# Local attention: both heads' probabilities transposed and copied first, their value products then issued in turn

## The chip, the cores and the metric

The kernel runs on one core of a Trainium2 chip. What counts is the device time of one execution in microseconds; the median of three runs of the kernel before is 2738.02 us (2737.78 to 2738.24). A core has five engines that run side by side and wait for each other through semaphores: TensorE (PE; its weight loads are listed as PEld), VectorE (DVE), ScalarE (ACT), GpSimd (POOL) and SyncE (SP, which here issues the DMAs). Each engine takes its own instructions in the order in which they stand in its queue.

## What is computed

A two-layer encoder block on 1024 tokens of width 1024. Each layer projects the tokens, runs three mixers side by side (differential attention over all keys with six heads, spatial gating, and a windowed attention with six query heads on two key heads), projects back, and adds a gated feed-forward part and a gated embedding part. The change is in the windowed ("local") attention:

```
def window_gqa(q, k, v, sinks, slopes):
    ...
    sc = jnp.where(valid[None, :, None, None], sc, NEG_INF)
    sink = sinks.astype(jnp.float32).reshape(SWA_KV_HEADS, SWA_GROUP)[:, :, None, None]
    m = jnp.maximum(jnp.max(sc, axis=-1, keepdims=True), sink)
    e = jnp.exp(sc - m)
    pr = e / (jnp.sum(e, axis=-1, keepdims=True) + jnp.exp(sink - m))
    o = jnp.einsum('bnkgqc,bnckd->bnqkgd', pr.astype(v.dtype), vb)
```

In the last line the probabilities of a block of 128 queries over its up to 384 keys are multiplied with the values of those keys.

## The kernel before

Tokens are cut into 8 blocks of 128. `swa(t, b)` does the local attention for query block t and two heads at once (g = 0 and 1, that is heads b and b + 3, one for each key head). It is called 24 times in each layer, 48 times in all. A block sees nk = 3 key blocks, the first and the last block nk = 2: 36 units with 384 columns and 12 with 256.

A unit goes through these steps. Scores for both heads on TensorE (L419), a bias, minimum and copy on VectorE (L425), the exponential on ScalarE (L428). Then, head after head: nk transposes of the probabilities on TensorE into a PSUM bank (L434), one copy of that bank to SBUF by ScalarE into a tile named PT (L436), and nk value products on TensorE (L438). A value product has 64 output rows: head 0 uses columns 0 to 63 of TensorE's array, head 1 columns 64 to 127 (in the profile the form 128\*64; a visit of this form is called a 64-column visit below). Each value product is fp32 and shows as two records. At the end the output goes to SBUF (L444), is transposed back (L446) and scaled by VectorE (L447).

`diff` is the differential attention, 48 calls a layer: scores (L481), VectorE (L484), ScalarE (L487), then per half of the keys four transposes (L503), a copy by ScalarE into a PT tile (L505), and value products (L509) that take the two column halves in turn by the key block's parity; L512 to L516 finish it. Its PT tiles, three buffers in all, and the two PSUM banks for transposes (4 and 5) are shared with `swa`.

A loop issues `diff` calls, `swa` calls and projection pieces (L238) by counts; but the order on each engine is made afterwards, by a scheduler that goes over the whole program with its own estimates of time. So an edit to one function moves instructions of its neighbours as well. Matrix products of the output projection (L220) follow at the end of the stage. The two layers have the same order in the parts shown here.

Of the kernel before, what the change touches and what calls it, by code (L numbers as in the profile page):

```python
# [16 lines left out]
AF = mybir.ActivationFunctionType  # L17
# [3 lines left out]
P = 128  # L21
# [36 lines left out]
def encoder_kernel(  # L58
# [7 lines left out]
    nc = tc.nc  # L66
# [6 lines left out]
    def nm(s):  # L73
        uid[0] += 1
        return f"{s}_{uid[0]}"

    def new(tag, shape, dt=F32):
        return sb.tile(shape, dt, tag=tag, name=nm(tag), bufs=BUFS[tag])

    def stat(k):  # L80
        if spos[0] + k > 224:
            spos[0] = 0
        spos[0] += k
        return stats[:, spos[0] - k : spos[0]]
# [4 lines left out]
    def pick(starts, width, hold):  # L89
        ok = [i for i in starts if not held & set(range(i, i + width))]  # L90
        i = min(ok, key=lambda j: max(stamp[j : j + width]))
        for j in range(i, i + width):
            stamp[j] = max(stamp) + 1
            if hold:
                held.add(j)
        return i

    def pbank2(hold=False):
        i = pick(SCORE_BANKS, 2, hold)
        return banks[:, i : i + 2]  # L100

    def pbank(among=range(4, 8), hold=False):
        i = pick(among, 1, hold)
        b = banks[:, i]
        bank_of[id(b)] = (i, b)
        return b
# [3 lines left out]
    def pfree(b):  # L110
        i = bank_of[id(b)][0]
        held.discard(i)
        stamp[i] = max(stamp) + 1
# [188 lines left out]
    for l in range(DEPTH):  # L302
# [40 lines left out]
        def vt(t, c0, n):  # L343
            c0 += (t % 2) * 512
            return V[:, t // 2, c0 : c0 + n]
# [31 lines left out]
        def c_view(t, b):  # L377
            return T(t)[:, 640 + P * b : 768 + P * b]
# [26 lines left out]
        def swa(t, b):  # L405
            k0, k1 = max(0, t - 1), min(NT, t + 2)
            nk = k1 - k0
            off = (k0 - t + 1) * P
            n = nk * P
            nmx, ssum = stat(2), stat(2)  # L410
            pr = new("G", [P, 2, 512])

            nc.gpsimd.tensor_copy(pr[:, :, n : n + 1], nsink[:, b : b + 4 : 3].unsqueeze(2))
            sc2 = pbank2()
            for g in range(2):
                h = b + 3 * g
                sc = sc2[:, g]
                rows = slice(64 * g, 64 * g + 64)
                nc.tensor.matmul(sc[:, :n], c_view(t, b)[rows], ck[0][rows, k0 * P : k1 * P],  # L419
                                 start=True, stop=True)  # L420
            for g in range(2):
                h = b + 3 * g
                sc = sc2[:, g]
                pg = pr[:, g, :n]
                nc.vector.tensor_tensor_reduce(pg, sc[:, :n], wtab[:, off : off + n], SWA_SLOPES[h],  # L425
                                               nsink[:, h : h + 1], ALU.add, ALU.min, nmx[:, g : g + 1])
                pg = pr[:, g, : n + 1]
                nc.scalar.activation(pg, pg, AF.Exp, bias=nmx[:, g : g + 1], scale=-1.0, accum_out=ssum[:, g : g + 1])  # L428
            yield
            po = pbank(AV_BANKS, hold=True)  # L430
            for g in range(2):
                pt = pbank(PT_BANKS)
                for j in range(nk):
                    nc.tensor.transpose(pt[:, j * P : (j + 1) * P], pr[:, g, j * P : (j + 1) * P], ident)  # L434
                pT_ = new("PT", [P, 512])
                nc.scalar.activation(pT_[:, :n], pt[:, :n], AF.Copy)  # L436
                for j in range(nk):
                    nc.tensor.matmul(po[64 * g : 64 * g + 64, 0:P],  # L438
                                     vt(k0 + j, 384 + 64 * g, 64), pT_[:, j * P : (j + 1) * P],
                                     start=(j == 0), stop=(j == nk - 1))  # L440
            rd = stat(2)
            nc.vector.reciprocal(rd, ssum)
            oT = new("O", [P, P])
            nc.scalar.activation(oT, po[:, 0:P], AF.Copy)  # L444
            pb = po[:, 256:384]
            nc.tensor.transpose(pb, oT, ident)  # L446
            nc.vector.tensor_tensor(c_view(t, b).rearrange("p (g d) -> p g d", g=2), pb.rearrange("p (g d) -> p g d", g=2),  # L447
                                    rd.unsqueeze(2).to_broadcast([P, 2, 64]), op=ALU.mult)
            pfree(po)
            yield  # L450
# [191 lines left out]
        for i in range(len(seq) + 2):  # L642
            if i < len(seq):
                h, t = seq[i]
                for hh in STACK_AT.get(i, ()):
                    slots[hh] = [stack(hh, 0), stack(hh, 1)]
                if i == GAINS_AT:
                    gpm = gain("G", g_post_mix, l)
                    gpf = gain("G", g_pre_ffn, l)
                g = diff(h, t, slots[h], i)  # L650
                next(g)
                pend.append((g, h, t))
                if i >= WO_AT:
                    load_wo(1)
                while nf < min(16, FILL_FIRST + 0.558 * (i + 1)):
                    next(fill)
                    nf += 1
                while ns < min(24, 0.629 * (i - 5)):
                    sg = swa(ns % 8, [int(f) for f in FILL if f in "012"][ns // 8])
                    next(sg)  # L660
                    spend.append(sg)
                    ns += 1
            while len(spend) > (1 if ns < 24 else 0):
                next(spend.pop(0))
            while pend and (len(pend) > 1 or i >= len(seq) + (len(pend) < 2)):
                g, h, t = pend.pop(0)
                next(g)
                if h == 5 and t >= MIX_LAG:
                    next(mix_step, None)
                if i >= len(seq):  # L670
                    break
# [254 lines left out]
```

## Time and profile before

| | |
|---|---|
| median of 3 runs | 2738.02 us |
| the profiled execution | 2735.23 us |
| its span | 2733.5 us |
| TensorE busy (PE) | 2675.9 us (98%) |
| weight loads (PEld) | 2154.2 us (79%) |
| VectorE busy | 1745.6 us (64%) |
| ScalarE busy | 1161.8 us (43%) |
| GpSimd busy | 323.1 us (12%) |

The span is the time from the first to the last instruction of the profiled execution. A TensorE matmul's busy time includes the time in which it runs beside the next one, so the busy times of single matmuls add up to more than the time that passes; the start of one block to the start of the next is what it takes. The local attention runs from 220 to 470 us (first layer) and from 1565 to 1805 us (second layer).

### The profile page before, as it was taken

The numbers are of one execution on the slowest core, as the hardware profiler recorded it, in microseconds if no ns is written. First come the engines' busy times: TensorE is split into PE (matmuls) and PEld (weight loads), VectorE is DVE, ScalarE is ACT, GpSimd is POOL, SyncE is SP. The second block draws the span as 40 slices with busy tenths as digits, with TensorE's granted clock in tenths as the row PEclk, the third lists the DMA queues.
The fourth block names the chain that finished last, engine by engine and source line by source line (L and its number), as shares of the span: only waits on it lengthen the run. The fifth ranks groups of instructions, "written<-read, shape, count | busy, mean of one in ns | idle before, by whom it ended". The sixth has DMA issues, their size and how long they took to land.

```text
span 2733.5 us, 35609 instructions
## 1 busy us (share of the span) xinstructions
PE 2675.9 (98%) x13760; PEld 2154.2 (79%) x13760; DVE 1745.6 (64%) x2944; ACT 1161.8 (43%) x1959; POOL 323.1 (12%) x299
## 2 busy tenths in 40 slices
PE   8999999999999999999999999999999999999998
PEld 6887776778888888887878777668788888888877
DVE  5237687568665646768632677866866666466684
ACT  6126788453222323124521577855433222321253
POOL 1002335210000000001100223532000000000010
PEclk9999999999999999999999999999999999999999
DMA  7153402133323214334224323012332232433332
GB/s 238 30 150 93 109 2 70 63 97 90 93 70 93 83 65 154 101 100 143 93 81 110 99 70 94 24 62 78 92 109 82 80 93 67 134 122 110 131 129 80
DMA packets 193465, 258.38 MB, mean 95 GB/s; under 512 B 26512, under 2 KB 142736, under 8 KB 193296
## 3 DMA queue, kind: packets, MB, share of 16 engines
q1 hardware_dynamic: 193296, 256.11, 30.5%
q8 instruction: 108, 1.77, 0.3%
q14 instruction: 61, 0.50, 0.1%
HBM read 195.25 MB, written 60.82 MB: 94 GB/s over the span
## 4 chain that ended last, share of the span: by engine, by line
PE 90%; DVE 6%; DMA 2%; issue 1%; ACT 1%; SPq 0%; POOL 0%; DVEq 0%; POOLq 0%; ACTq 0%
PE banks L714 30%; PE banks L220 17%; PE banks L793 16%; PE banks L238 8%; PE banks L509 3%; PE banks L503 3%; PE banks L481 3%; PE banks L438 2%; PE banks L202 2%; PE banks L266 1%; PE banks L419 1%; PE banks L434 1%; DVE A L196 1%; PE banks L515 1%; DMA raw<-in_w_in_dram 1%
## 5 line engine op out<-in xcount | busy, mean ns | idle before, releaser
L714 PE MATMUL banks<-A,W 128*128 128x512 f32 x3072 | 710.5, 391 | 7.2 <-ACT W L161 4.9
L714 PEld LDWEIGHTS banks<-A,W 128*128 128x128 f32 x3072 | 579.2, 189 | 131.3 <-ACT W L161 6.4
L220 PE MATMUL banks<-W,A 128*128 128x512 f32 x1728 | 420.6, 396 | 12.0 <-ACT A L209 6.4
L220 PEld LDWEIGHTS banks<-W,A 128*128 128x128 f32 x1728 | 322.8, 190 | 81.3 <-ACT A L209 7.6
L799 DVE TENSOR_TENSOR A<-banks,A 128x512 f32<-128x512 f32 x320 | 213.9, 687 | 111.7 <-PE banks L793 111.4
L793 PE MATMUL banks<-W,F 128*128 128x512 f32 x1152 | 263.7, 389 | 0.0
L793 PEld LDWEIGHTS banks<-W,F 128*128 128x128 f32 x1152 | 216.2, 188 | 44.9
L793 PE MATMUL banks<-W,W 128*128 128x512 f32 x960 | 220.0, 389 | 1.8 <-ACT W L161 1.8
L161 ACT ACTIVATE W<-G 128x1024 fp32r<-128x1024 f32 x88 | 92.5, 1060 | 296.8 <-PE banks L714 279.0
L189 POOL TENSOR_TENSOR stats<-stats,neghalf 128x1 f32<-128x1 f32 (+1 forms) x112 | 84.8, 759 | 1095.7 <-DVE stats L187 1094.6
L793 PEld LDWEIGHTS banks<-W,W 128*128 128x128 f32 x960 | 180.1, 188 | 39.4 <-ACT W L161 2.0
L161 ACT ACTIVATE W<-raw 128x1024 fp32r<-128x1024 f32 x92 | 96.7, 1059 | 209.6 <-PE banks L793 100.7
L238 PE MATMUL banks<-A,F 128*128 128x512 f32 x768 | 183.8, 393 | 0.0
L738 DVE TENSOR_TENSOR P<-banks,P 128x512 f32<-128x512 f32 x44 | 30.4, 690 | 219.7 <-PE banks L714 219.7
L238 PEld LDWEIGHTS banks<-A,F 128*128 128x128 f32 x768 | 142.1, 188 | 29.5 <-issue 0.7
L484 DVE CUSTOM_DVE_ANT_0 P<-banks,dist 128x1024 f32<-128x1024 f32 x116 | 139.9, 1218 | 36.2 <-PE banks L481 22.8
L220 PE MATMUL banks<-F,A 128*128 128x512 f32 x576 | 148.0, 400 | 0.7 <-DVE stats L484 0.7
L487 ACT ACTIVATE P<-P,stats 128x1024 f32<-128x1024 f32 x116 | 133.0, 1148 | 28.7 <-DVE stats L484 26.9
L162 DVE TENSOR_TENSOR W<-raw,W 128x1024 fp32r<-128x1024 f32 x80 | 97.6, 1223 | 52.6 <-ACT W L161 52.5
L714 PE MATMUL banks<-A,raw 128*128 128x512 f32 x528 | 126.8, 389 | 0.0
L220 PEld LDWEIGHTS banks<-F,A 128*128 128x128 f32 x576 | 107.4, 191 | 23.2 <-issue 1.0
L505 ACT ACTIVATE PT<-banks 128x512 f32<-128x512 f32 x192 | 111.2, 590 | 22.2 <-PE banks L503 18.0
(192 smaller groups left out, 3888.0 us busy)
## 6 DMA issues: line engine op xcount, KB each, us to landing
F<-in_w_ffn_in_dram SPq DMA_DIRECT2D x88, 512.0 KB, 5.1
f<-P SPq DMA_DIRECT2D x44, 512.0 KB, 4.5
raw<-f SPq DMA_DIRECT2D x44, 512.0 KB, 3.3
raw<-in_w_ffn_out_dram SPq DMA_DIRECT2D x44, 512.0 KB, 3.5
W<-pre SPq DMA_DIRECT2D x64, 256.0 KB, 5.2
pre<-G SPq DMA_DIRECT2D x24, 512.0 KB, 3.6
x<-A SPq DMA_DIRECT2D x24, 512.0 KB, 2.6
e<-G SPq DMA_DIRECT2D x16, 512.0 KB, 4.9
```

What stands on the lines that cost most here:

```text
L161: nc.scalar.activation(hi, src, AF.Copy)
L162: eng.tensor_tensor(lo, src, hi.bitcast(F32), op=ALU.subtract)
L189: nc.gpsimd.tensor_tensor(r, v, neghalf[:, :k], op=ALU.pow)
L220: nc.tensor.matmul(ps[:, hf], x[a][:, k * P : (k + 1) * P], units[k][b][:, hf * 512 : (hf + 1) * 512], start=(k == 0 and a == 0 and b == 0 ...
L238: nc.tensor.matmul(po, w[a][:, k * P : (k + 1) * P], X[half][b][:, :, k * P : (k + 1) * P], start=(k == 0 and a == 0 and b == 0), stop=(k ...
L481: nc.tensor.matmul(sc[:, hf], slots[c][:, 0, t * P : (t + 1) * P], slots[c][:, 1, hf * 512 : (hf + 1) * 512], start=True, stop=True)
L484: nc.vector.tensor_tensor_reduce(pc, sc.rearrange("p a b -> p (a b)"), dist[:, 896 - 128 * t : 1920 - 128 * t], DIFF_SLOPES[h], HUGE, ALU. ...
L487: nc.scalar.activation(pc, pc, AF.Exp, bias=nmx[:, c : c + 1], scale=-1.0, accum_out=s[:, c : c + 1])
L505: nc.scalar.activation(pT_, pt, AF.Copy)
L714: nc.tensor.matmul(bank, w[i][a][:, k * P : (k + 1) * P], B[i][:, b, k * 512 : (k + 1) * 512], start=k == 0 and a + b == 0, stop=k == 3 an ...
L793: nc.tensor.matmul(po, fs[i][a][:, t * P : (t + 1) * P], ws[i][b][:, hf * 512 : (hf + 1) * 512], start=(i == 0 and a == 0 and b == 0), sto ...
L799: nc.vector.tensor_tensor(acc, po, acc, op=ALU.add)
```

## The change

In `swa` the second half is cut in two: first both heads are transposed and copied, then all value products are issued, key block by key block, the two heads in turn. Head 0's copy stays on ScalarE; head 1's is done by VectorE.

```
             po = pbank(AV_BANKS, hold=True)
+            pT_ = []
             for g in range(2):
                 pt = pbank(PT_BANKS)
                 for j in range(nk):
                     nc.tensor.transpose(pt[:, j * P : (j + 1) * P], pr[:, g, j * P : (j + 1) * P], ident)
-                pT_ = new("PT", [P, 512])
-                nc.scalar.activation(pT_[:, :n], pt[:, :n], AF.Copy)
-                for j in range(nk):
+                pT_.append(new("PT", [P, 512]))
+                if g == 0:
+                    nc.scalar.activation(pT_[g][:, :n], pt[:, :n], AF.Copy)
+                else:
+                    nc.vector.tensor_copy(pT_[g][:, :n], pt[:, :n])
+
+            for j in range(nk):
+                for g in range(2):
                     nc.tensor.matmul(po[64 * g : 64 * g + 64, 0:P],
-                                     vt(k0 + j, 384 + 64 * g, 64), pT_[:, j * P : (j + 1) * P],
+                                     vt(k0 + j, 384 + 64 * g, 64), pT_[g][:, j * P : (j + 1) * P],
                                      start=(j == 0), stop=(j == nk - 1))
```

The lines behind the edit move down by six: the scores of `diff` are L487 and L490, its transposes L509, its products L515 in the new kernel; the local products are L444, the copies L438 (ScalarE) and L440 (VectorE), the local transposes L435.

The order of instructions, first on TensorE, at one unit late in the first layer's local attention (about 442 to 447 us of the profile). G is the tile of probabilities, PT a copied transpose, A_600 the values, ident the unit matrix, W and P the tiles of `diff`. Before:

```order
L434 MATMUL banks<-ident,G_3616 128x128 x3
L481 MATMUL banks<-A_2660 128x512 x2
L438 MATMUL banks<-PT_3741,A_600 64x128 x3
L503 MATMUL banks<-ident,P_3672 128x128 x4
L515 MATMUL banks<-fold,O_3711 128x64
L481 MATMUL banks<-A_2660 128x512 x2
L438 MATMUL banks<-PT_3749,A_600 64x128 x3
```

After, from the second head's transposes on:

```order
L435 MATMUL banks<-ident,G_3616 128x128 x3
L487 MATMUL banks<-A_2660 128x512 x2
L444 MATMUL banks<-PT_3741,A_600 64x128
L509 MATMUL banks<-ident,P_3672 128x128 x3
L521 MATMUL banks<-fold,O_3711 128x64
L509 MATMUL banks<-ident,P_3672 128x128
L444 MATMUL banks<-PT_3746,A_600 64x128
L444 MATMUL banks<-PT_3741,A_600 64x128
L444 MATMUL banks<-PT_3746,A_600 64x128
L444 MATMUL banks<-PT_3741,A_600 64x128
L444 MATMUL banks<-PT_3746,A_600 64x128
```

Two blocks of three products have become one single product and a block of five that takes the heads in turn. In other units the six stand together.

On VectorE, at the same unit, after the change (P and stats are tiles of `diff`, G_3801 is the next unit's tile of probabilities):

```order
L490 ISA P_3787,stats<-banks,dist 128x1024
L490 ISA stats 128x1
L518 COPY O_3711<-banks 128x128
L440 COPY PT_3746<-banks 128x384
L425 ISA G_3801,stats<-banks,wtab,lay_575 128x384
```

The copy of the second head's transposes (L440) is new there; it stands behind a score pass of `diff` (L490) and ahead of a score pass of the next unit (L425).

Counted over the whole order, both layers: TensorE's visits of the 64-column form were 209 and are 199, groups of local score matmuls (L419) were 46 and are 50, and blocks of local products of one head and of both heads were as follows.

| local products, blocks standing alone | before | after |
|---|---|---|
| three of one head | 40 | 0 |
| two of one head | 12 | 0 |
| three and three, head after head | 12 | 0 |
| two and two, head after head | 4 | 0 |
| six in turn | 0 | 16 |
| five in turn | 0 | 18 |
| four in turn | 0 | 6 |
| three in turn | 0 | 4 |
| one | 0 | 20 |

Eight blocks before and six after adjoin a block of the differential attention's products instead.

## Rows read from the trace of the kernel before

**Rows 1.** The page: busy us of each engine with its share of the span and its instructions; then the shares by engine of the chain of work that ended last.

```profile
PE 2675.9 (98%) x13760; PEld 2154.2 (79%) x13760; DVE 1745.6 (64%) x2944; ACT 1161.8 (43%) x1959; POOL 323.1 (12%) x299
...
PE 90%; DVE 6%; DMA 2%; issue 1%; ACT 1%; SPq 0%; POOL 0%; DVEq 0%; POOLq 0%; ACTq 0%
```

**Rows 2.** The table of windows: stretch in us from the span's start, its length, then for each engine (PE, PEld, DVE, ACT, POOL) busy us with the count of instructions, and last the granted TensorE clock, the DMA share and GB/s. Four short windows, the part of the first stage with projections, the dense parts of both stages and the end of the first stage.

```profile
200.00:220.00 20.00, 19.50 (x147) 15.09 (x145) 18.42 (x35) 14.76 (x26) 5.32 (x3) 1.00 0.26 80
340.00:360.00 20.00, 20.00 (x169) 14.62 (x167) 18.67 (x48) 17.59 (x41) 7.31 (x6) 1.00 0.01 2
420.00:440.00 20.00, 19.44 (x149) 12.82 (x149) 16.01 (x40) 19.11 (x39) 14.01 (x9) 1.00 0.31 81
1680.00:1700.00 20.00, 20.00 (x165) 14.21 (x164) 18.95 (x48) 17.86 (x38) 5.48 (x7) 1.00 0.01 2
220.00:340.00 120.00, 119.96 (x836) 90.95 (x836) 79.97 (x201) 81.75 (x173) 35.58 (x29) 1.00 0.41 106
340.00:400.00 60.00, 59.49 (x481) 42.63 (x481) 52.92 (x141) 53.57 (x119) 21.02 (x18) 1.00 0.01 2
400.00:460.00 60.00, 59.28 (x471) 41.56 (x469) 48.28 (x124) 52.65 (x112) 35.58 (x25) 1.00 0.18 45
460.00:510.00 50.00, 43.61 (x244) 32.50 (x245) 30.27 (x57) 21.69 (x45) 13.28 (x9) 0.90 0.16 53
1660.00:1760.00 100.00, 98.98 (x810) 70.49 (x809) 86.34 (x225) 88.38 (x194) 40.38 (x32) 1.00 0.13 30
1760.00:1800.00 40.00, 37.05 (x282) 25.71 (x282) 31.71 (x77) 32.75 (x70) 24.96 (x16) 1.00 0.32 91
```

**Rows 3.** The timeline of TensorE, 442 to 454 us: start, us from the first start to the last end, engine, line, operation, tiles, shapes and records.

```profile
442.22 0.66 PE L509 MATMUL banks<-PT,A 128*64 128x128 f32 x8
442.81 0.55 PE L434 MATMUL banks<-ident,G 128*128 128x128 f32 x3
...
443.75 0.87 PE L438 MATMUL banks<-PT,A 128*64 128x128 f32 x6
444.55 0.66 PE L503 MATMUL banks<-ident,P 128*128 128x128 f32 x4
...
446.63 0.66 PE L503 MATMUL banks<-ident,P 128*128 128x128 f32 x4
447.12 0.49 PE L434 MATMUL banks<-ident,G 128*128 128x128 f32 x3
...
447.65 1.09 PE L509 MATMUL banks<-PT,A 128*64 128x128 f32 x16
448.68 0.55 PE L434 MATMUL banks<-ident,G 128*128 128x128 f32 x3
...
452.69 0.66 PE L503 MATMUL banks<-ident,P 128*128 128x128 f32 x4
453.27 0.66 PE L509 MATMUL banks<-PT,A 128*64 128x128 f32 x8
```

**Rows 4.** The same view at two other places: a unit with both heads' products side by side (253.91 us), and one head of a unit with two key blocks (337.92 us); behind each the block that follows.

```profile
253.91 1.15 PE L438 MATMUL banks<-PT,A 128*64 128x128 f32 x12
254.98 0.66 PE L503 MATMUL banks<-ident,W 128*128 128x128 f32 x4
...
337.92 0.65 PE L438 MATMUL banks<-PT,A 128*64 128x128 f32 x4
338.50 0.66 PE L503 MATMUL banks<-ident,P 128*128 128x128 f32 x4
```

**Rows 5.** Groups of instructions by line and form: tiles, shapes and count, busy us, mean ns of one, idle time before and who ended it. L484 is the score pass, L436 the copies of the local attention on ScalarE, L512 a small copy from PSUM on VectorE, L373 a pass of VectorE over 512 columns of PSUM.

```profile
L484 DVE CUSTOM_DVE_ANT_0 P<-banks,dist 128x1024 f32<-128x1024 f32 x116 | 139.9, 1218 | 36.2 <-PE banks L481 22.8 <-POOL P L495 7.6 <-PE banks L503 5.0
...
L436 ACT ACTIVATE PT<-banks 128x384 f32<-128x384 f32 x72 | 35.0, 485 | 6.4 <-PE banks L434 3.3 <-PE banks L509 3.1
...
L512 DVE COPY O<-banks 128x128 f32<-128x128 f32 x82 | 23.2, 283 | 8.3 <-PE banks L509 8.2
...
L436 ACT ACTIVATE PT<-banks 128x256 f32<-128x256 f32 x24 | 9.0, 373 | 4.2 <-PE banks L434 4.0
...
L373 DVE TENSOR_TENSOR G<-banks,G 128x512 fp32r<-128x512 f32 x12 | 8.3, 690 | 22.9 <-ACT G L372 22.9
```

**Rows 6.** The table of windows for L436 alone: ScalarE's busy us and its copies (two for each unit) in the four dense parts, then the clock and DMA columns.

```profile
340.00:400.00 60.00, 6.57 (x14) 1.00 0.01 2
400.00:460.00 60.00, 6.06 (x13) 1.00 0.18 45
1660.00:1760.00 100.00, 9.96 (x23) 1.00 0.13 30
1760.00:1800.00 40.00, 4.88 (x11) 1.00 0.32 91
```

**Rows 7.** The timeline of TensorE at the end of the first stage; in brackets the idle time before an instruction and who ended it.

```profile
464.24 0.73 PE L481 MATMUL banks<-A 128*128 128x512 f32 x2 [2.02 <-DVE stats L484]
...
495.03 0.73 PE L481 MATMUL banks<-A 128*128 128x512 f32 x2 [1.28 <-DVE A L196]
497.43 1.22 PE L481 MATMUL banks<-A 128*128 128x512 f32 x2 [1.67 <-DVE stats L484]
498.58 1.98 PE L509 MATMUL banks<-PT,A 128*64 128x128 f32 x16
500.49 4.37 PE L220 MATMUL banks<-F,A 128*128 128x512 f32 x12
```

## The prediction

> **What bounds the kernel now.** I read the page first: how busy each engine is and what the chain that ended last consists of. TensorE is busy for 2675.9 of 2733.5 us and makes up 90% of that chain, VectorE 6%, ScalarE 1% [rows 1]. So the end moves only by what TensorE no longer has to do, or by what it newly has to wait for. Then I read the table of windows over the two attention stages, where the edited function runs, because a share over the whole span hides what happens there. In the first part of a stage projection matmuls lie between the attention steps: in 220 to 340 us TensorE is busy for 119.96 of 120 us, VectorE and ScalarE for about two thirds. Then come dense parts (340 to 460 us, 1660 to 1800 us) in which all three are nearly full: in 340 to 400 us TensorE 59.49, ScalarE 53.57, VectorE 52.92 of 60 us [rows 2]. TensorE is the bound there too, but the cover is thin. The edit takes work from the fullest engine and hands a copy from the second to the third.
>
> **TensorE: the value products.** Matmuls overlap, so a block's cost is not its busy time but the step from its first start to the start of the next block, read off the timeline. Each value product is two records. One head's three products (6 records) start at 443.75 us and the next block at 444.55: 0.80 us. The differential attention, whose products already alternate between the two column halves of the array, takes 0.59 us for 8 records (442.22 to 442.81) and 1.03 us for 16 (447.65 to 448.68) [rows 3]. Hence two products on different halves cost 0.22 us together, which is also what one product on one half costs (2 products of one head take 0.58 us, [rows 4]); besides, every visit of the 64-column form has a fixed 0.15 us in its block. Alternating heads is therefore the real gain. It is smaller where both heads' products already stand side by side, unmixed: that block of 12 records takes 1.07 us (253.91 to 254.98), not 1.60, because its second half starts before the first is done [rows 4].
>
> Now the count, from the order of TensorE's instructions, both layers together. Before there are 40 blocks of three products (0.80), 12 of two (0.58), 12 of both heads with three each (1.07) and 4 with two each (0.60, taken as the 0.59 of the like block); 8 more adjoin a block of the other attention and cost 0.15 less or so: four threes (0.75), two sixes (0.94), two fours (0.49), estimates. Sum 32.0+7.0+12.8+2.4+5.9 = 60.1 us. After, an alternating block costs 0.15 us and 0.22 us for each product on its fuller half: 16 blocks of six and 18 of five (0.81 each), 6 of four and 4 of three (0.59), 20 of one (0.37), and 6 adjoining ones (two of six at 0.67, two of four at 0.48, two of one at 0.33: 3.0). Sum 27.5+5.9+7.4+3.0 = 43.8 us. The saving is 16.3 us. Those 20 single ones are a flaw of the new order: the first head's first product goes ahead alone as soon as ScalarE has copied, another block follows, and then come the other five.
>
> The scheduler also regroups the neighbours. Visits of the 64-column form fall from 209 to 199, six of them in the differential attention, whose fixed 0.15 us is thus saved 6 times (0.9 us). Entering a visit costs about 0.09 us: four transposes before one take 0.58 us, before other transposes 0.49 us [rows 3]; 10 entries are 0.9 us. Score matmuls of this function are split into 50 groups instead of 46, which I put at 0.3 us each, an estimate from the fixed cost and the entry just named: 1.2 us back. TensorE's work falls by about **17 us**, 0.35 us for each of the 48 units.
>
> At this point a rule speaks against the change. The trace shows the two halves working at the same time: 16 records in 1.03 us against 6 in 0.80 [rows 3]. The Trainium skill, TensorE: Matmul & The Clock Gate, Part 3 (Packing small matmuls), says that a weight load overlaps running matmuls only when its row group differs; both halves here use all rows, so by it they would go one after the other. The blocks of 16 records contradict it. What it would cost is the second rival.
>
> **The copies.** The first head's stays on ScalarE, the second's goes to VectorE: 48 copies, 36 of 384 columns and 12 of 256. ScalarE is relieved of 36 x 0.485 + 12 x 0.373 = 21.9 us [rows 5], which nobody waits for by itself. The trace has no VectorE copy of this size; the bounds are the 128-column copy from PSUM (0.28 us) and the 512-column pass (0.69 us), between which the slope is 1.06 ns a column, so 0.55 and 0.42 us [rows 5], **24.8 us in all**. Their cover is TensorE's other work: between the second head's transposes and its first product there stand at least 1.3 us of it in every unit, by the order and the steps above. In the shown unit the copy stands behind a score pass of 1.22 us and a small copy on VectorE, and ahead of two score passes of the local attention, on which later transposes depend.
>
> So does VectorE still keep up? Copies by window (ScalarE's, halved, [rows 6]) give 7 units in 340 to 400 us, 6.5 in 400 to 460, 11.5 in 1660 to 1760 and 5.5 in 1760 to 1800. With 0.52 us more for each on VectorE and 0.35 us less on TensorE, VectorE would need 56.5 of 57.5 us (98%), 51.7 of 57.7 (90%), 92.3 of 96.0 (96%) and 34.6 of 38.1 (91%), ScalarE less than now. It stays below full on average, so it doesn't become the bound outright, but every late score pass reaches TensorE. What that costs isn't in the trace at this load; the nearest rows are 20 us windows with a second engine at 92 to 96%: two lost 0.50 and 0.56 us of TensorE, two lost nothing [rows 2]. The four stretches lose 0.51, 0.72, 1.02 and 2.95 us of TensorE as they are, 5.2 us together [rows 2]. The bounds for new stalls are thus nothing (as in the two windows without loss) and, from the other side, 15 us, where nearly the whole gain is gone; I let the stretches lose twice what they lose now, **5 us** more, since their load rises to that of the windows that lost something. The first 9 and 7 units lie beside projections and give their 0.35 us undiminished.
>
> **The end of the stage.** Around and after the last unit TensorE waits for VectorE's score and norm passes: 2.02 us before 464.24, 1.28 before 495.03 and 1.67 before 497.43, and the granted clock over 460 to 510 us is 0.90 [rows 2, 7]; at 498.58 a block of 16 records takes 1.91 us instead of 1.03. These depend on VectorE's chain and are in both orders; one score step moves ahead of them. I put zero for them, with 2 us either way. DMA issues keep their order but for one gain load that passes a weight load.
>
> **Sum.** 17 - 5 = 12 us less: 2723 us for the profiled execution (2735.23 us, of which 2733.5 is the span). The median of the three runs, 2738.02, is 2.8 us above it, so I forecast **2726.0 us**.
>
> **The rivals.** *VectorE takes it back*: late copies and score passes eat nearly the whole gain. For it: 98% in one stretch, and VectorE's one queue, where a copy that waits for transposes holds up the score passes behind it. Against: at least 1.3 us of slack, and stretches at 93 to 95% without loss. Each dense unit (some 31) would have to lose 0.5 us instead of 0.16: 17 - 15, or 2736 us. *The halves don't work together in this order*, so that the change doesn't do what it says: at 0.22 us each after 0.15, six products would take 1.47 us, five 1.25, four 1.03, three 0.81. 18 sixes, 18 fives, 8 fours, 4 threes and 22 single ones make 68 us for 60: 8 us more, less 1 for visits, plus the 5 us of stalls, or 2750 us. Against it stands the differential attention's block, in the same form. (The rule of the Trainium skill named above would give this case.) *The copy is always late (the slower side)*: a unit whose products find the copy not done stops TensorE, with the other attention's transposes queued behind them. From 17/48 = 0.35 us per unit on, the change loses; at 0.5 us in all 48, with the clock falling at two more places for 2 us each, it is 24 + 4 - 17 = 11 us slower, 2749 us.
>
> **How the numbers follow.** Forecast, a gain of 8 to 19 us: 0.70. VectorE takes it back, a gain of 0 to 8 us: 0.21. The two slower cases together 0.09, 0.03 of it for halves that don't pair; 0.01 of them I leave within the bound. A measurement of this kernel can tell about 0.2% (5.5 us) from no change; the bound for faster is thus 2732.5 us, and I put 0.07 of the second case beyond it: faster 0.77, same 0.15, slower 0.08. The range goes from 2717 (all of the work, 2 us at the end, no stall) to 2737 (the second case whole).
>
> **What would show it.** Right: blocks of local products with 10 and 12 records that step on after 0.81 us; VectorE copies of 0.55 us; ScalarE near 22 us less busy; TensorE's stalls in 340 to 460 us at 2 to 4 us, put down to VectorE. Wrong: alternating blocks of 1.2 us or more; TensorE's idle time before its local products or score matmuls grown by 15 us with VectorE named; copies of over 1 us while GpSimd works.

## The result and the profile after

The change is faster: 2720.21 us (2719.19 to 2723.65, 4 runs) against 2737.95 us, a ratio of 0.9936 [0.9924, 0.9949], or 17.7 us less. The profiled execution took 2721.15 us, its span 2719.4 us; before it was 2733.5 us. So 14.1 us of the gain can be looked for in the two traces. The other 3.6 us lie in which execution was profiled: before, it ran 2.7 us under the median, after, 0.9 us over it.

The page of the changed kernel, to be read against [rows 1]:

```profile
span 2719.4 us, 35553 instructions
...
PE 2660.4 (98%) x13760; PEld 2140.7 (79%) x13760; DVE 1757.5 (65%) x2992; ACT 1143.2 (42%) x1911; POOL 319.3 (12%) x299
...
PE 91%; DVE 4%; ACT 2%; issue 1%; DMA 1%; POOL 1%; SPq 0%; DVEq 0%; POOLq 0%; ACTq 0%
```

TensorE is busy for 15.5 us less (2675.9 to 2660.4) and idle for 1.4 us more (57.6 to 59.0, span less busy time). The chain is still TensorE's. ScalarE lost 18.6 us of work that had hardly been on the chain, VectorE got 11.9 us more (its new copies take 24.9; its other passes take less or lie beside them).

The timeline of TensorE in the unit whose order stands ahead of the prediction, and in one whose six products stand together (start, us to the last end, engine, line, operation, tiles, shapes, records):

```profile
438.39 0.43 PE L444 MATMUL banks<-PT,A 128*64 128x128 f32 x2
438.76 0.55 PE L509 MATMUL banks<-ident,P 128*128 128x128 f32 x3
...
439.52 0.87 PE L444 MATMUL banks<-PT,A 128*64 128x128 f32 x10
440.32 0.66 PE L509 MATMUL banks<-ident,P 128*128 128x128 f32 x4
...
254.72 0.88 PE L444 MATMUL banks<-PT,A 128*64 128x128 f32 x12
255.53 0.43 PE L521 MATMUL banks<-fold,O 128*128 128x64 f32 x2
```

A single product steps on after 0.37 us, the other five after 0.80, six together after 0.81. In [rows 3] three products of one head alone took 0.80, in [rows 4] six head after head 1.07. The other blocks are like these: all 16 of six take 0.81 us, all 18 of five 0.80, all 20 single ones 0.36 to 0.37.

The table of windows over the dense parts, to be read against [rows 2] (the kernel is ahead by then, so the later windows hold slightly later work; columns as there):

```profile
340.00:400.00 60.00, 59.13 (x506) 41.81 (x506) 57.98 (x156) 52.93 (x118) 22.09 (x19) 1.00 0.01 1
400.00:460.00 60.00, 57.55 (x482) 40.41 (x483) 52.41 (x134) 50.01 (x105) 34.72 (x23) 0.99 0.26 70
400.00:450.00 50.00, 49.42 (x417) 34.49 (x417) 42.85 (x113) 43.61 (x90) 30.51 (x21) 1.00 0.21 54
450.00:500.00 50.00, 43.86 (x273) 33.70 (x270) 31.97 (x67) 25.18 (x52) 15.35 (x11) 0.90 0.18 54
1650.00:1750.00 100.00, 98.59 (x832) 68.76 (x831) 92.03 (x244) 86.73 (x187) 40.60 (x33) 1.00 0.15 35
```

VectorE is as full as the prediction had it, 57.98 of 60 us or 97%, and yet TensorE loses only 0.87 us there (0.51 before). In 400 to 460 us it loses 2.45 us (0.72 before), but 1.87 of them are the first two waits below; before, the waits around the last unit (0.74 and 2.02 us) stood behind that window, at 460.62 and 464.24 us. TensorE in the change at the end of the first stage:

```profile
456.47 0.73 PE L487 MATMUL banks<-A 128*128 128x512 f32 x2 [1.32 <-DVE stats L490]
...
457.86 0.63 PE L509 MATMUL banks<-ident,P 128*128 128x128 f32 x4 [0.55 <-DVE PT L440]
...
486.67 0.74 PE L487 MATMUL banks<-A 128*128 128x512 f32 x2 [1.94 <-DVE A L196]
489.07 0.86 PE L487 MATMUL banks<-A 128*128 128x512 f32 x2 [1.67 <-DVE stats L490]
```

The copies, by form:

```profile
L440 DVE COPY PT<-banks 128x384 f32<-128x384 f32 x36 | 19.9, 553 | 7.2 <-PE banks L515 5.3 <-PE banks L435 1.4 <-PE banks L452 0.5
...
L440 DVE COPY PT<-banks 128x256 f32<-128x256 f32 x12 | 5.0, 415 | 0.3
```

0.553 and 0.415 us, where 0.55 and 0.42 were worked out: 24.9 us in all. In each of the 48 units this copy ends at least 0.37 us before head 1's first product starts, and no matmul among those products waits for it.

### The profile page after: what moved, and what is told of

It reads as the page before. It is cut to its first block, busy times and chain, and to the rows that moved or that the text cites. A ratio compares the mean times of both kernels' runs of the same rounds, so it can differ in the third digit from the quotient of the medians.

```text
span 2719.4 us, 35553 instructions
## 1 busy us (share of the span) xinstructions
PE 2660.4 (98%) x13760; PEld 2140.7 (79%) x13760; DVE 1757.5 (65%) x2992; ACT 1143.2 (42%) x1911; POOL 319.3 (12%) x299
## 4 chain that ended last, share of the span: by engine, by line
PE 91%; DVE 4%; ACT 2%; issue 1%; DMA 1%; POOL 1%; SPq 0%; DVEq 0%; POOLq 0%; ACTq 0%
PE banks L720 30%; PE banks L220 18%; PE banks L799 17%; PE banks L238 8%; PE banks L515 3%; PE banks L487 3%; PE banks L509 3%; PE banks L202 2%; PE banks L266 2%; PE banks L419 1%; PE banks L444 1%; PE banks L435 1%; PE banks L521 1%; DVE A L196 1%; DVE P L490 1%
## 5 line engine op out<-in xcount | busy, mean ns | idle before, releaser
L490 DVE CUSTOM_DVE_ANT_0 P<-banks,dist 128x1024 f32<-128x1024 f32 x116 | 139.8, 1219 | 32.5 <-PE banks L487 19.2
```

The lines of the kernel that those rows point to most:

```text
L490: nc.vector.tensor_tensor_reduce(pc, sc.rearrange("p a b -> p (a b)"), dist[:, 896 - 128 * t : 1920 - 128 * t], DIFF_SLOPES[h], HUGE, ALU. ...
```

## Experiments

All runs were timed against the kernel before on the same chip. Two versions whose ratios differ by 0.002 or less (some 5 us) have overlapping intervals, so such a difference is a hint and not shown. First the changed kernel was taken apart.

**Products in turn alone.** Both copies stay on ScalarE:

```
-                if g == 0:
-                    nc.scalar.activation(pT_[g][:, :n], pt[:, :n], AF.Copy)
-                else:
-                    nc.vector.tensor_copy(pT_[g][:, :n], pt[:, :n])
+                nc.scalar.activation(pT_[g][:, :n], pt[:, :n], AF.Copy)
```

> Products in turn as in the change, but both copies on ScalarE. Theory P (TensorE's work in the 64-column form sets the time): counted from its order with the steps of the trace before (0.22 us a pair, 0.15 us fixed and 0.15 us for entering a visit), that form costs 182.7 us, against 195.5 in the kernel before and 177.0 in the changed one. So 13 us less work than before, less 2 to 5 us of new stalls: 2727 to 2730 us. Theory S (the gain comes from taking 22 us of copies off ScalarE): no gain, 2738 us. Theory O (the scheduler's other regrouping made the gain): nothing definite, anything from 2720 to 2738.

Measured: 2725.70 us, ratio 0.9956 [0.9942, 0.9969], so 11.9 us less than before. Theory P had set 8 to 11, theory S none. TensorE is busy for 9.3 us less than before, where P counted 13, and 6.2 us more than in the change: with both copies on ScalarE the order has 214 visits of the 64-column form, against 199 in the change.

**The copy alone.** Copies as in the change, products head after head:

```
-            for j in range(nk):
-                for g in range(2):
+            for g in range(2):
+                for j in range(nk):
```

> The second head's copy on VectorE and both copies ahead of the products, as in the change, but the products head after head. Theory P: the 64-column form costs 189.2 us by its order, 6 us less than before (more blocks of both heads side by side, 10 visits fewer), less 3 to 5 us of stalls from VectorE's 25 us of copies: 2735 to 2738 us. Theory S: as fast as the change, 2720 us.

Measured: 2730.30 us, 0.9970 [0.9958, 0.9981], 7.3 us less than before: more than P gave, far from the 17.7 of S. TensorE's busy time fell by 9.9 us and its idle time rose by 2.0, so this gain too shows as TensorE's work (both heads' products side by side in 16 blocks instead of 12, 199 visits instead of 209). P had both terms wrong: 6 us of work and 3 to 5 us of stalls.

**Both heads on one column half.** The products alternate, but head 1's go to the same 64 columns:

```
-                    nc.tensor.matmul(po[64 * g : 64 * g + 64, 0:P],
+                    nc.tensor.matmul(po[0:64, g * P : (g + 1) * P],
...
-            nc.scalar.activation(oT, po[:, 0:P], AF.Copy)
+            for g in range(2):
+                nc.scalar.activation(oT[64 * g : 64 * g + 64], po[0:64, g * P : (g + 1) * P], AF.Copy)
```

> As the change, but both heads' products go to the same 64 columns of the array (head 1's result to other columns of the PSUM bank), so that they can't run beside each other; ScalarE then copies the result in two pieces, 48 small copies of about 0.27 us more. Theory P: 209.3 us in the 64-column form, 14 us more than before, plus 5 us of stalls: 2752 to 2760 us, blocks of six at 1.47 us. Theory S: some 13 us of ScalarE lost again, 2720 to 2728 us. If the products in turn didn't overlap anyway, as fast as the change.

Measured: 2743.48 us, 1.0020 [1.0012, 1.0029], 5.9 us slower than before. TensorE's timeline of this run:

```profile
440.24 1.31 PE L444 MATMUL banks<-PT,A 128*64 128x128 f32 x10
441.48 0.66 PE L510 MATMUL banks<-ident,W 128*128 128x128 f32 x4
```

Five products step on after 1.24 us instead of 0.80, in all 22 such blocks, and six after 1.46 instead of 0.81, in all 12. So it is the two halves working together that pays, and not the turn in itself. (ScalarE's 48 small copies come on top, but TensorE's busy time alone rose by more than the whole loss.) The sign and the step are P's; its size was not: TensorE's busy time rose by 10.5 us where 14 were counted, and its idle time fell by 2.4 instead of rising by 5 (57.6 to 55.2). That a longer TensorE gives the others more time would fit this; it is not shown.

**Head 1 first.** Each pair begins with the head whose copy comes last:

```
             for j in range(nk):
-                for g in range(2):
+                for g in (1, 0):
```

> As the change, but each pair of products begins with head 1, whose copy comes last, so that no single product goes ahead alone: 32 blocks of six instead of 16, nearly no singles, 190 visits of the 64-column form instead of 199. Theory P: 170.3 us in that form, 7 us less than the change, if stalls stay alike: 2712 to 2716 us. Theory S: as the change, 2720 us. Rival for this run: the singles filled time in which TensorE would have waited, so that the stalls grow by the same 7 us: 2720 us.

Measured: 2716.53 us, 0.9922 [0.9908, 0.9935], some 4 us under the change; the two intervals overlap. The single products are nearly gone and TensorE's busy time is 6.7 us below the change's (7 were counted), but its idle time is 3.7 us above it. The largest wait, 10.4 us in both layers together, sits in one place, once in each layer. TensorE and VectorE there in this run:

```profile
451.17 0.27 PE L452 MATMUL banks<-ident,O 128*128 128x128 f32 x1
456.64 1.12 PE L444 MATMUL banks<-PT,A 128*64 128x128 f32 x8 [5.21 <-DVE PT L440]
```

```profile
449.14 2.44 DVE L534 TENSOR_TENSOR PT<-A,stats 128x384 f32<-128x384 f32 x1
...
453.20 3.06 DVE L503 SCALAR_TENSOR_TENSOR P<-P,stats,P 128x1024 f32<-128x1024 f32 x1
456.18 0.41 DVE L440 COPY PT<-banks 128x256 f32<-128x256 f32 x1
```

The last unit's copy stands on VectorE behind a normalization pass that took 2.44 us and a combination that took 3.06. GpSimd in the same stretch:

```profile
448.80 2.37 POOL L162 TENSOR_TENSOR W<-raw,W 128x1024 fp32r<-128x1024 f32 x1
451.15 1.42 POOL L500 TENSOR_SCALAR P<-P,stats 128x1024 f32<-128x1024 f32 x1
452.66 2.52 POOL L501 TENSOR_TENSOR P<-P,P 128x1024 f32<-128x1024 f32 x1
```

The two slow passes run beside these GpSimd passes and end 0.4 and 1.1 us after one of them. In this run none of the 34 combinations (L503) and 10 normalization passes (L534) that no GpSimd pass touches took over 1.29 and 0.56 us. The PSUM copies don't show this: in the change none took over 0.56 us, and 28 of the 48 lie beside a GpSimd pass.

**That copy moved.** Head 1 first, with the last unit's second copy on ScalarE:

```
-                if g == 0:
+                if g == 0 or (t, b) == (NT - 1, 1):
```

> As the run with head 1 first, but the last unit of each layer has both copies on ScalarE. The order on every engine is else the same (VectorE's differs by one row a layer). In that run TensorE waited 5.2 us a layer for the last copy, which stood on VectorE behind a normalization pass of 2.4 us and a combination of 3.1 us, both two to four times their usual length while GpSimd worked. Theory Q (that one place in VectorE's queue costs 10 us in all, clock included): 2706 to 2709 us. Rival (the same late VectorE passes then hold up the score matmuls behind it instead): 2713 to 2717 us.

Measured: 2715.06 us, 0.9921 [0.9907, 0.9934]: the same ratio as with the copy on VectorE. TensorE's order is the same, instruction for instruction. The rival was right, and the wait has only changed its name:

```profile
453.09 0.33 PE L452 MATMUL banks<-ident,O 128*128 128x128 f32 x1 [0.37 <-ACT O L450]
457.79 1.22 PE L487 MATMUL banks<-A 128*128 128x512 f32 x2 [4.37 <-DVE stats L490]
```

Score matmuls now wait at 457.79 us for the same VectorE queue.

Then came runs that set VectorE's and ScalarE's load or the order further off.

**Both copies on VectorE**, in the change:

```
-                if g == 0:
-                    nc.scalar.activation(pT_[g][:, :n], pt[:, :n], AF.Copy)
-                else:
-                    nc.vector.tensor_copy(pT_[g][:, :n], pt[:, :n])
+                nc.vector.tensor_copy(pT_[g][:, :n], pt[:, :n])
```

> As the change, but both copies on VectorE: 22 to 25 us more for VectorE and 21 us less for ScalarE than in the change, 180.2 us in the 64-column form (3 us more than the change). Theory V (VectorE, at 90 to 98% in the dense parts by the forecast, is next to bind and its load comes back as stalls): over 100% in the dense parts, so at least 10 us of new stalls, 2733 us or more. Theory F (the stalls belong to the fixed chain at the end of the stage and hardly to VectorE's load): 2722 to 2725 us.

Measured: 2728.50 us, 0.9968 [0.9956, 0.9981], between the two theories. TensorE's idle time is 64.4 us, 5.4 more than in the change; a wait for a copy, once in each layer, is 4.8 us long (us in total, times, longest):

```profile
PE banks L441 <- DVE PT L437: 9.6, 2, 4.8
```

**Engines changed over**, head 0's copy on VectorE:

```
-                if g == 0:
+                if g == 1:
                     nc.scalar.activation(pT_[g][:, :n], pt[:, :n], AF.Copy)
```

> As the change with the engines changed over: head 0's copy, the early one, on VectorE and head 1's on ScalarE. 175.2 us in the 64-column form by its order, 2 us less than the change; loads alike. Theory P: 2717 to 2720 us. Rival (the place of the copy in VectorE's queue decides): off by more than 5 us either way.

Measured: 2729.18 us, 0.9972 [0.9961, 0.9984], 9 us behind the change with like loads. 2 us less work were counted, but TensorE is busy for 2.3 us more than in the change; its idle time is 65.3 us, 6.3 more. So P fails here in its count and in its stalls. The rival's range holds; that the copy's place in the queue is the reason isn't shown, since the order of all engines changed with it.

**Head 1 first, all copies on ScalarE**; the edit joins the first and the fourth experiment's.

> Head 1 first and all copies on ScalarE: VectorE's load as before the change, 164.7 us in the 64-column form, 31 us less than before the change and 6 us less than the run with head 1 first. If VectorE's load makes the stalls, they fall to the level of the kernel before, and it takes 2707 to 2711 us. If ScalarE's queue makes as many, 2715 us or more.

Measured: 2728.90 us, 0.9968 [0.9956, 0.9981]. VectorE's load is that of the kernel before (1742.9 us), so it is not an added load of VectorE that makes these stalls. TensorE's busy time is 23.7 us below the kernel before's (31 were counted), but idle time is 13.0 us up, at 70.6. Moving the second copy to VectorE is thus worth 12 us in this order (2728.90 to 2716.53), and some 5.5 in the change's (2725.70 to 2720.21), where the intervals overlap. Whom TensorE waited for in this run:

```profile
PE banks L484 <- DVE stats L487: 8.2, 7, 2.0
...
PE banks L518 <- DVE O L515: 5.7, 2, 2.8
...
PE banks L419 <- DVE stats L487: 4.3, 4, 1.6
...
PE banks L512 <- ACT PT L508: 2.6, 6, 0.7
```

In 220 to 475 and 1544 to 1810 us, where the local attention runs, 18.1 us of TensorE's waits end with VectorE and 4.6 with ScalarE, though all the copies stand on ScalarE.

**All eight products of the differential attention together**, on top of head 1 first:

```
             for hf in range(2):
...
-                pT_ = new("PT", [P, 512])
-                nc.scalar.activation(pT_, pt, AF.Copy)
-                for j in range(4):
-                    kt = hf * 4 + j
...
+                pT_.append(new("PT", [P, 512]))
+                nc.scalar.activation(pT_[hf], pt, AF.Copy)
+            for kt in (4, 5, 6, 7, 0, 1, 2, 3):
...
```

> The run with head 1 first, and in the differential attention too both halves are transposed and copied (on ScalarE as before) ahead of all eight products, those of the second half first. Nearly all its blocks become blocks of eight: 140 visits of the 64-column form instead of 199, 154.6 us in it instead of 177.0 in the change and 195.5 before. Theory P, if a quarter of the saving goes into stalls as in the runs so far: 17 us under the change, some 2703 to 2707 us. Rival (stalls fill up what is saved, since VectorE's chain is then what the dense parts take): 2714 us or more.

Measured: 2720.95 us, 0.9940 [0.9927, 0.9954], 4 us behind head 1 first alone, with overlapping intervals, and in the rival's range (2714 or more). The page of this run, and whom TensorE waited for (us in total, times, longest):

```profile
PE 2643.5 (97%) x13760; PEld 2143.3 (79%) x13760; DVE 1759.2 (65%) x2992; ACT 1143.9 (42%) x1911; POOL 323.4 (12%) x299
```

```profile
PE banks L487 <- DVE stats L490: 10.6, 12, 2.3
PE banks L444 <- DVE PT L440: 10.5, 4, 5.0
PE banks L515 <- ACT PT L512: 7.5, 14, 0.7
```

TensorE is busy for 32.4 us less than in the kernel before (41 were counted) and idle for 20.0 us more. Its idle time is no longer in a single place alone: score matmuls wait for VectorE 12 times, the products 14 times for ScalarE's copies.

**Weight splits on VectorE.** The low halves of the output projection's weights go from GpSimd to VectorE, in the version that ended best (head 1 first, last copy on ScalarE) and in the change:

```
-                    wo.append(rows_unit("F" if k < 2 else "W", w_out[l], k, nc.gpsimd))
+                    wo.append(rows_unit("F" if k < 2 else "W", w_out[l], k, nc.vector))
...
-                                                             704 + 64 * (k - 5) + 192 * g, :]) for g in range(2)], nc.gpsimd))
+                                                             704 + 64 * (k - 5) + 192 * g, :]) for g in range(2)], nc.vector))
```

> As the run with head 1 first and the last unit on ScalarE, but the low halves of the output projection's weights (16 passes of 1024 columns, 2.4 us each on GpSimd) are made on VectorE (1.2 us each, 20 us more for it). 169.6 us in the 64-column form, as there. If VectorE's passes over two SBUF operands lose more by waiting for GpSimd than they cost, it takes 2707 to 2711 us; if VectorE's own load is what TensorE waits for, 2718 us or more.

> The change as it is, with the same split of weights on VectorE. 176.9 us in the 64-column form, as in the change. VectorE, at 97% in 340 to 400 us of the changed kernel, gets 20 us more between some 300 and 490 us of each layer's like stretch, 10 us a layer. If its load comes back as stalls, 2725 us or more; if the stalls come from single places and not from load, 2718 to 2722 us.

Measured: 2716.36 us, 0.9921 [0.9907, 0.9934], and 2724.28 us, 0.9949 [0.9935, 0.9962]. The first is level with its base, neither as good as hoped nor as bad as feared; the second is 4 us behind the change, with overlapping intervals, and between its two cases. The normalization pass, in the kernel before (L528) and in the first of these runs (L534; ns: shortest, median, longest):

```profile
L528 DVE TENSOR_TENSOR PT<-A,stats x16: 546/558/1967, 458.4 to 1904.7; 128x384 f32<-128x384 f32 x16
...
L534 DVE TENSOR_TENSOR PT<-A,stats x16: 546/559/726, 456.1 to 1885.6; 128x384 f32<-128x384 f32 x16
```

With these passes off GpSimd the longest falls from 2.45 us to 0.73, which bears out that the two engines get in each other's way there. But taking the passes off gains no time in either version.

TensorE's busy and idle time by the pages (idle is span less busy) beside the times:

| kernel | busy, against before | idle | median us | ratio |
|---|---|---|---|---|
| before | 2675.9 | 57.6 | 2737.95 | 1 |
| the change | -15.5 | 59.0 | 2720.21 | 0.9936 |
| in turn alone | -9.3 | 61.7 | 2725.70 | 0.9956 |
| copy alone | -9.9 | 59.6 | 2730.30 | 0.9970 |
| one column half | +10.5 | 55.2 | 2743.48 | 1.0020 |
| head 1 first | -22.2 | 62.7 | 2716.53 | 0.9922 |
| the same, last copy on ScalarE | -23.6 | 61.0 | 2715.06 | 0.9921 |
| both copies on VectorE | -12.7 | 64.4 | 2728.50 | 0.9968 |
| engines changed over | -13.2 | 65.3 | 2729.18 | 0.9972 |
| head 1 first, all on ScalarE | -23.7 | 70.6 | 2728.90 | 0.9968 |
| head 1 first, eight together | -32.4 | 77.6 | 2720.95 | 0.9940 |
| head 1 first, last copy on ScalarE, splits on VectorE | -22.2 | 60.3 | 2716.36 | 0.9921 |
| change, splits on VectorE | -14.2 | 60.8 | 2724.28 | 0.9949 |

Busy and idle come from one execution each, the medians from several, so the two differ by a few us; most in the turn alone, profiled 4.4 us above its median, and in head 1 first with all on ScalarE, 4.3 below.

## Why the prediction was right, and where it was off

**TensorE's work: right.** The steps of the blocks came out as set (0.81, 0.80 and 0.37 us). The steps of all 64-column visits add up to 16.6 us less than before, and busy time fell by 15.5 us where 17 were counted. That the turn across the two halves makes most of the gain is shown by the run on one half, in which it is lost, and by the run with the turn alone, which keeps two thirds of it; the copy alone, head after head, keeps 7.3 us, and that too as TensorE's work. The way of counting was less sure than this: the counts in the expectations (with 0.15 us for entering a visit, where the prediction took 0.09) came out 3.0 us too high in the change and 2.6 to 4.4 in most other versions, but 7.1 to 8.5 with the engines changed over, with all on ScalarE and with eight together, and 3.6 too low in the copy alone.

By the Trainium skill (TensorE: Matmul & The Clock Gate, Part 3) a weight load overlaps running matmuls only when its row group differs. The trace disagrees: weight loads take 2154.2 us of a span in which matmuls take 2675.9 of 2733.5 [rows 1], so most of them run beside a matmul, and nearly all are of forms that use all 128 rows. That two column halves would go one after the other was the second rival's own step from that rule, and it failed: five products cost 0.80 us on two halves and 1.24 on one. In the blocks that take the halves in turn two records start together (0.007 us apart) every 0.109 us; on one half a single one does.

**The copies: right in length, wrong in what moving them does.** 0.553 and 0.415 us as worked out, and they had cover in every unit. ScalarE's busy time fell by 18.6 us where near 22 were set. The prediction took ScalarE's relief as something that nobody waits for by itself, and the copy on VectorE as a cost alone. But with both copies on ScalarE the same products in turn gave 11.9 us instead of 17.7, and the order with head 1 first lost 12 us. In the change's order this shows as TensorE's work (6.2 us more, 214 visits instead of 199): with the copy on the other engine the scheduler makes another order. In the other order it shows as idle time (70.6 us against 62.7), ended mostly by VectorE. ScalarE was next to full in the dense parts [rows 2], but that its load was the reason is not shown by either.

**The stalls: the mis-sized term.** I took 5 us, "twice what they lose now". TensorE's idle time rose by 1.4 us. From the first to the last local score matmul it rose by 1.6 us in both layers together (2.4 to 4.0). VectorE's load was forecast well for 340 to 400 us (98%, measured 97%; in 400 to 460 it was 87% for 90), but TensorE lost 0.87 us there, where twice the 0.51 was set. The sign set for 340 to 460 us, stalls of 2 to 4 us, came true with 3.3 us, but only because waits of the stage's end had moved into that window. The four 20 us windows that the size was read from couldn't give it: the fuller engine was at 92 and 96% in the two that lost something and at 93 and 95% in the two that lost nothing. Of the difference between forecast (12) and profile (14.1), 1.5 us less work and 3.6 us less stalls make up the 2.1; the two errors have opposite signs and partly cancel, which was luck. The rest up to the median's 17.7 is the two profiled executions' place among their runs. The low end of the range, 2717, is not what its terms give: all of the work and 2 us at the end, taken from 2738.02, make 2719; the measured time lies above both.

**The end of the stage: right.** The waits there are alike in kind (1.94 and 1.67 us before the two last score matmuls, 1.28 and 1.67 in [rows 7]), and the granted clock is 0.90 over 450 to 500 us, as it was over 460 to 510.

**The rivals.** That VectorE takes it back didn't happen in the change. It did with a further twist: changing the engines over cost 6.3 us of idle time at like load, and eight products together 20.0 us of idle time over the kernel before. Halves that don't pair: refuted in the change; with one half in their place the kernel is 5.9 us slower, where the rival had 12. The copy always late: refuted, since no product waited for it. In the change a copy on VectorE ended a wait of a TensorE matmul in one place a layer, at 457.86 us for 0.55 us, and that one stood before transposes of the differential attention.

**What stays open.** Why the changed-over engines stall so much more than the change, and why VectorE comes late with all copies on ScalarE, is not settled: the scheduler puts out another order for each version, and only in the run with the last copy moved was the order held still. Whether GpSimd's passes cost anything on the whole is open too, since moving them loads VectorE.

## What to carry to other kernels

Where products fill only half of TensorE's columns, issue two that fill different halves in turn; count the blocks in the order that the scheduler made, and price them by start-to-start steps of a like block in the trace. The steps held to 0.01 us here; the work counted from them was right within 1.5 us in the change and up to 8.5 us off in the other versions, where the neighbours are regrouped in other ways. Begin such a run with the operand that comes last, so that none goes ahead alone: that took 6.7 us more off TensorE's work, of which some 4 us of time is a hint and not shown. Once TensorE's cover is thin, less work on it can turn into waiting, and how much is not told by the work: with 22 to 24 us taken off, 3 to 13 came back as idle time, with 32 taken off, 20.

## What I had not expected

A VectorE 97% full over 60 us cost TensorE only 0.87 us there. And a stage can lose idle time when TensorE gets more work: with 10.5 us more, 2.4 us of idle time went. A normalization pass of VectorE over two SBUF operands took 2.44 us beside GpSimd's work, where the same pass has a median of 0.56 us (and a longest of 1.97) in the kernel before.
